# A hybrid mLSTM and sparse-attention block on one core: two sets of transposes alternate between PSUM rings, and one output chunk changes its issuing engine

## The chip, the cores and the metric

The kernel runs on 1 core of one Trainium2 chip. The metric is the device time of one execution in microseconds (us). Three runs of the kernel before gave 654.09, 654.55 and 655.37 us; the median is 654.55 us. A further execution was taken by the profiler; its rows are the ones quoted below.

## The reference, cut to what matters

The block takes `x` (256 tokens of width 2048), normalises it, and projects it into everything that two parallel groups of heads need. At the end it multiplies by gates, projects back, adds a gated per-token embedding and normalises again.

```python
h = rmsnorm(x, norm_g[l])
(mq, mk, mv, mo, mz, mi, mf, nq, kc, vc, ks, vs, kw, vw, ng, nz) = split_cols(h @ w_in[l], IN_SPLITS)
...
hm = head_layernorm(hm, m_norm_g[l]).astype(x.dtype)
m_out = hm * jax.nn.sigmoid(mo) * jax.nn.silu(mz)
q = partial_rope(heads(nq, N_HEADS) * (N_HEAD_DIM ** -0.5), positions)
n_att = nsa_mixer(q, ...)
...
x = x + jnp.concatenate([m_out, n_out], axis=-1) @ w_out[l]
ple = rmsnorm(p[l] @ ple_proj_w[l], ple_norm_g[l])
x = x + jax.nn.sigmoid(x @ ple_gate_w[l]) * ple
return rmsnorm(x, final_norm_g)
```

Two tensors matter here: `q`, the 16 attention heads of 64 that the sparse attention reads, and `hm`, the 4 mLSTM heads of 256 that go, gated, into the output projection. TensorE needs both with the feature on the partitions, so both are transposed on it.

## The kernel before

**Tiles and stages.** All weights come as a stream of 512 KB pieces (units, class `Unit`). Each is loaded by SyncE's DMA queue (line 157), split by ScalarE into a high part `whi` (line 166) and by VectorE into a low part `wlo` (line 167), and multiplied three times: `x_hi*w_hi`, `x_lo*w_hi`, `x_hi*w_lo` (line 193; lines 178 and 181 where the features are on the partitions). These products (`mainps`) fill TensorE. Everything else, the attention, the mLSTM and the gates, is written as Python generators (`tracks`) whose pieces are laid between the units.

**What sets the order.** The order of every engine is the order of the Python code (`manual_schedule`), and each engine works it off strictly. One turn of the main loop emits: the evacuation of a block that ended in the turn before, the load of unit i+4, the split of unit i+3, the products of unit i, and then `advance()`, which lets every live track go on to its next `yield`. A track that yields after its transposes has their evacuation in the next turn, behind that turn's products on TensorE.

**PSUM.** It has 8 banks of 2 KB per partition, dealt out in rings by tag: `main` 3 banks (`main_ps`), `aux` 2 tiles of one bank (`aux`), `wide` 1 tile of two banks (`wide`), `acc` 1. A new tile of a ring may be written when the tile that had its place has been read for the last time; the framework puts that wait on the first TensorE instruction that writes it.

**Queries.** In `nsa` (from line 602) the loop over `h0` handles four heads a turn: 4 transposes (line 625) into two `aux` tiles, then, one turn later, 4 copies by ScalarE (line 614) and 4 subtractions by VectorE (line 619), which read both tiles and write the high and the low part of `qT`. There are 4 such groups, called here q1 to q4, one unit apart. After q4 come the scores of the compressed keys, 2 x 16 small products (line 631), into `psc`, which is a `wide` tile of two banks.

**Mixed heads.** In `gate_m` (from line 1048) the gated `hm` is transposed in groups of 4 (line 1067) into one `aux` tile of one bank each; ScalarE (line 1070) and VectorE (line 1072) evacuate it in the next turn, two instructions each. There are two such tracks, for the two halves of the features, one turn apart, so the four groups come in the order m1 (second half, `k0` = 4), m2 (first half, `k0` = 0), m3 (second half, `k0` = 6), m4 (first half, `k0` = 2); m2 and m3 fall into the same turn and m4 into the next one.

**The end.** The last product block is cut into three (`EDGES`), the second half of the tokens last. `write(t)` (lines 1256 to 1268) scales four chunks of 128 x 512 in the order of columns 1, 0, 3, 2: chunk 1 by VectorE (line 1265), 0 and 2 by ScalarE (line 1267), 3 by VectorE (line 1263). Each is issued to memory by SyncE (line 1268). `write(1)` is the last thing that the program does.

Of the kernel before, what the change touches and what calls it, by code (L numbers as in the profile page):

```python
# [19 lines left out]
S = 256  # L20
# [79 lines left out]
def hybrid_block(ctx, tc, x, xT, pT, positions, wst, cols, w1in, ple_norm_g, final_norm_g, out):  # L100
    nc = tc.nc
# [11 lines left out]
    def aux(shape, dt=F32):  # L113
        return psum.tile(shape, dt, name="auxps", tag="aux", bufs=2)

    def wide(shape):
        return psum.tile(shape, F32, name="wideps", tag="wide", bufs=1)

    def t2(shape, dt=F32, name="t2"):
        return tmp.tile(shape, dt, name=name, tag="t2", bufs=5)  # L120
# [233 lines left out]
    def rope(xv, nh):  # L354
        tt = (t4 if nh > NG else t2)([128, 2, T, nh, ROT], name="rope")
        a, b = tt[:, 0], tt[:, 1]
        c = cos16.rearrange("p t a b -> p t (a b)")
        V.tensor_tensor(a, xv[:, :, :, 0:ROT], c[:, :, None, :].to_broadcast([128, T, nh, ROT]), OP.mult)
        V.tensor_tensor(b[:, :, :, 0:HALF], xv[:, :, :, HALF:ROT],
                        nsin[:, :, None, :].to_broadcast([128, T, nh, HALF]), OP.mult)  # L360
        V.tensor_tensor(b[:, :, :, HALF:ROT], xv[:, :, :, 0:HALF],
                        sin8[:, :, None, :].to_broadcast([128, T, nh, HALF]), OP.mult)
        V.tensor_tensor(xv[:, :, :, 0:ROT], a, b, OP.add)
# [238 lines left out]
    def nsa():  # L602
        nonlocal natt, qT
        while "cmp" not in done:
            yield
        qT = tmp.tile([128, NH, S], F32R, name="qT", tag="qT")
        rope(q.rearrange("p t (h d) -> p t h d", d=ND), NH)
        yield
        prev = None
        for h0 in range(0, NH + 4, 4):  # L610
            if h0:
                for a in range(2):
                    for c in range(2):
                        A.copy(qT[0:ND, h0 - 4 + 2 * a + c], prev[a][c * ND:(c + 1) * ND])
                for a in range(2):
                    for c in range(2):
                        h = h0 - 4 + 2 * a + c
                        src = prev[a][c * ND:(c + 1) * ND]
                        V.tensor_tensor(qT[ND:128, h], src, qT[0:ND, h].bitcast(F32), OP.subtract)
            if h0 < NH:  # L620
                prev = [aux([128, S]) for _ in range(2)]
                for a in range(2):
                    for t in range(T):
                        c0 = (h0 + 2 * a) * ND
                        PE.transpose(prev[a][:, t * 128:(t + 1) * 128], q[:, t, c0:c0 + 2 * ND], ident)
                yield
        natt = tmp.tile([128, NW // 128, S], F32, name="natt", tag="q8")
        psc = wide([128, T, NH, 2, NC16])
        for t in range(T):
            for h in range(NH):  # L630
                PE.matmul(psc[:, t, h].rearrange("p a c -> p (a c)"), qT[:, h, t * 128:(t + 1) * 128],  # L631
                          kcmpT[:, h // NJ].rearrange("p a c -> p (a c)"), start=True, stop=True)
            yield
        pc = t2([128, T, NJ, NG, NC16], name="pc")
        for t in range(T):
            sc = psc[:, t].rearrange("p (g j) a c -> p g j a c", g=NG)
            pg = pc[:, t].rearrange("p j g c -> p g j c")
            V.tensor_tensor(pg, sc[:, :, :, 0], cadd[:, t, None, None, :].to_broadcast([128, NG, NJ, NC16]), OP.add)
            V.tensor_tensor(pg, sc[:, :, :, 1], pg, OP.add)
        tracks.append(cmp_probs(pc))  # L640
        while not {"k0", "k1", "vw"} <= done:
            yield
        yield from attend_all()

    def cmp_probs(pc):
        nonlocal pcT
        pcT = tmp.tile([128, T, NJ, 128], F32R, name="pcT", tag="pcT")
        cst = tmp.tile([128, 2, T, NJ, NG], F32, name="cst", tag="cst")
        a0, a1 = (cst[:, i].rearrange("p t j g -> p (t j g)") for i in range(2))
        pcf = pc.rearrange("p t j g c -> p (t j g) c")  # L650
        V.tensor_reduce(a0, pcf, axis=AX.X, op=OP.max)
        V.tensor_tensor(pcf, pcf, a0[:, :, None].to_broadcast([128, T * NH, NC16]), OP.subtract)
        yield
        A.activation(pcf, pcf, AF.Exp)
        yield
        V.tensor_reduce(a1, pcf, axis=AX.X, op=OP.add)
        V.reciprocal(a1, a1)
        for t in range(T):
            pt = pc[:, t].rearrange("p j g c -> p (j g) c")
            V.tensor_tensor(pt, pt, cmul[:, t, None, :].to_broadcast([128, NH, NC16]), OP.mult)  # L660
        yield
        while "vw" not in done:
            yield
        V.tensor_tensor(cst[:, 1].rearrange("p t j g -> p t g j"), cst[:, 1].rearrange("p t j g -> p t g j"),
                        gates[:, :, :, 0].rearrange("p t (g j) -> p t g j", g=NG), OP.mult)
        V.tensor_tensor(pcf, pcf, a1[:, :, None].to_broadcast([128, T * NH, NC16]), OP.mult)
        yield
        yield
        H = NG * NC16
        for t in range(T):  # L670
            ps = psum.tile([H, NJ, 128], F32, name="pcps", tag="acc", bufs=1)
            for j in range(NJ):
                PE.transpose(ps[:, j], pc[:, t, j].rearrange("p g c -> p (g c)"), ident)
            yield
            A.copy(pcT[0:H, t], ps)
            V.tensor_tensor(pcT[H:128, t], ps, pcT[0:H, t].bitcast(F32), OP.subtract)
            yield
        done.add("pcT")
# [354 lines left out]
    def ev_mz(i):  # L1033
        def f(ps):
            tzs = []
            for t in range(T):
                tz = t2([128, 512], name="tz")
                A.activation(tz, ps[t], AF.Tanh, scale=rh[:, t:t + 1])
                zc = t2([128, 512], name="zc")
                A.copy(zc, ps[t])  # L1040
                V.scalar_tensor_tensor(tz, tz, 1.0, zc, op0=OP.add, op1=OP.mult)
                tzs.append(tz)
            tracks.append(gate_m(i, tzs))
        return f
# [3 lines left out]
    def gate_m(i, tzs):  # L1048
        nonlocal mixm
        for t in range(T):  # L1050
            sl = gmt[:, t, i * 512:(i + 1) * 512]
            V.scalar_tensor_tensor(sl, sl, 1.0, tzs[t], op0=OP.add, op1=OP.mult)
            yield
        while "mlstm" not in done:
            yield
        for t in range(T):
            hs = hm[:, t, 2 * i:2 * i + 2].rearrange("p h d -> p (h d)")
            V.tensor_tensor(hs, hs, gmt[:, t, i * 512:(i + 1) * 512], OP.mult)
            yield
        if i == 0:  # L1060
            mixm = tmp.tile([128, 2, KT // 2, S], F32R, name="mixm", tag="qk")
        hf = hm.rearrange("p t h d -> p t (h d)")
        for k0 in range(4 * i, 4 * i + 4, 2):
            ps = aux([128, 2, S])
            for j in range(2):
                for t in range(T):
                    PE.transpose(ps[:, j, t * 128:(t + 1) * 128], hf[:, t, (k0 + j) * 128:(k0 + j + 1) * 128], ident)
            yield
            for j in range(2):
                A.activation(mixm[:, 0, k0 + j], ps[:, j], AF.Copy, scale=mgcol[:, k0 + j:k0 + j + 1])  # L1070
            for j in range(2):
                V.scalar_tensor_tensor(mixm[:, 1, k0 + j], ps[:, j], mgcol[:, k0 + j:k0 + j + 1],
                                       mixm[:, 0, k0 + j].bitcast(F32), op0=OP.mult, op1=OP.subtract)
        done.add(f"mix{i}")
# [181 lines left out]
    def write(t):  # L1256
        f = frr[:, t:t + 1]
        o = out[0, t * 128:(t + 1) * 128]
        for c in (1, 0, 3, 2):
            sl = slice(c * 512, (c + 1) * 512)  # L1260
            xx = x2[t][:, sl]
            if c == 3:
                V.scalar_tensor_tensor(xx, xx, f, fgb[:, sl], op0=OP.mult, op1=OP.mult)
            elif c == 1:
                V.tensor_scalar(xx, xx, f, None, op0=OP.mult)
            else:
                A.activation(xx, xx, AF.Copy, scale=f)
            nc.sync.dma_start(o[:, sl], xx)


    halves = [(t, a, a + 512) for a in (512, 0) for t in range(T)]
# [27 lines left out]
    ps = wide([128, 2, 128])  # L1299
# [77 lines left out]
```

## Time and profile before

| what | value |
|---|---|
| median of 3 runs | 654.55 us (654.09 to 655.37) |
| the profiled execution, its own time | 655.25 us |
| its span, first to last instruction | 653.5 us |
| TensorE busy | 638.0 us, 98% of the span |
| VectorE busy | 467.0 us, 71% |
| ScalarE busy | 378.8 us, 58% |
| GpSimd busy | 62.2 us, 10% |
| mean granted TensorE clock, share of full speed | 0.996 |

The profiled execution's own time holds its span and 1.75 us around it; it lies 0.7 us above the median of the three runs and inside their spread. A row of the timeline reads: start in us from the span's start, us from its first start to its last end, engine, line of the kernel, operation, what it writes and reads, shape, count, and in brackets the idle time of the engine before it and what ended that. PE is TensorE's products, PEld its weight loads (a transpose has one of each), DVE is VectorE, ACT ScalarE, POOL GpSimd, SPq SyncE's queue.

### The profile page before, as it was taken

What the parts mean: (1) busy time and instruction counts of PE and PEld (TensorE: products, weight loads), DVE (VectorE), ACT (ScalarE), POOL (GpSimd) and SP (SyncE); (2) the same over time, 40 slices, a digit from 0 to 9 for tenths busy, and PEclk for the clock granted to TensorE, in tenths of its full rate; (3) what the DMA queues carried; (4) which work ended last, traced back from release to release, by engine and by line L of the source; (5) the groups of instructions that cost most, each with busy time, mean ns of one, the idle gap of its engine ahead of it and who ended that gap; (6) DMA issues with size and microseconds to landing.
All of it is one profiled execution on the core that took longest, in us unless ns stands there. A gap on an engine that the chain in (4) does not pass through costs nothing.

```text
span 653.5 us, 9104 instructions
## 1 busy us (share of the span) xinstructions
PE 638.0 (98%) x3287; PEld 550.6 (84%) x3287; DVE 467.0 (71%) x712; ACT 378.8 (58%) x655; POOL 62.2 (10%) x70
## 2 busy tenths in 40 slices
PE   7999999999999999999999999999999999999994
PEld 6889999898888888888888888887888888888884
DVE  4669877877776657799998776787755765545564
ACT  5678844746565655767765656677634433444442
POOL 0002240000111112111110000010000000022430
PEclk9999999999999999999999999999999999999998
DMA  8996555546545445454456653455688665556633
GB/s 294 354 345 203 173 149 157 178 149 197 162 161 161 144 147 161 134 157 128 143 180 187 195 185 127 130 178 166 198 286 286 225 210 189 175 181 195 193 95 130
DMA packets 35902, 121.04 MB, mean 185 GB/s; under 512 B 4240, under 2 KB 5008, under 8 KB 35344
## 3 DMA queue, kind: packets, MB, share of 16 engines
q1 hardware_dynamic: 34704, 115.98, 55.9%
q10 hardware_dynamic: 1152, 4.47, 1.9%
q8 instruction: 26, 0.43, 0.3%
q14 instruction: 20, 0.16, 0.1%
HBM read 118.33 MB, written 2.10 MB: 184 GB/s over the span
## 4 chain that ended last, share of the span: by engine, by line
PE 94%; DVE 2%; DMA 1%; issue 1%; ACT 1%; SPq 0%; POOL 0%; ACTq 0%; POOLq 0%; DVEq 0%
PE mainps L193 61%; PE mainps L178 13%; PE mainps L181 7%; PE wideps L193 3%; PE wideps L692 2%; PE auxps L738 2%; DMA wraw<-in_wst_dram 1%; PE po L771 1%; PE po L769 1%; PE wideps L970 1%; PE auxps L441 1%; PE auxps L1204 1%; PE auxps L945 1%; PE wideps L631 1%; ACT whi L166 0%
## 5 line engine op out<-in xcount | busy, mean ns | idle before, releaser
L167 DVE TENSOR_TENSOR wlo<-wraw,whi 128x1024 fp32r<-128x1024 f32 (+3 forms) x214 | 257.8, 1206 | 151.1 <-ACT whi L166 149.0
L166 ACT CAST whi<-wraw 128x1024 fp32r<-128x1024 f32 (+3 forms) x214 | 216.4, 1013 | 183.6 <-PE mainps L193 123.7
L193 PE MATMUL mainps<-whi,hT 128*128 128x512 f32 (+2 forms) x704 | 182.5, 377 | 0.5 <-DVE vst L527 0.3
L193 PEld LDWEIGHTS mainps<-whi,hT 128*128 128x128 f32 x704 | 128.3, 188 | 17.9 <-ACT whi L166 0.8
L178 PE MATMUL mainps<-hT,whi 128*128 128x512 f32 x384 | 105.6, 396 | 0.0
L193 PE MATMUL mainps<-wlo,hT 128*128 128x512 f32 (+2 forms) x352 | 105.0, 373 | 0.5 <-DVE wlo L167 0.5
L178 PEld LDWEIGHTS mainps<-hT,whi 128*128 128x128 f32 x384 | 66.2, 189 | 9.5
L193 PEld LDWEIGHTS mainps<-wlo,hT 128*128 128x128 f32 x352 | 65.6, 188 | 9.9 <-DVE wlo L167 1.0
L193 PE MATMUL mainps<-whi,x2T 128*128 128x512 f32 (+1 forms) x288 | 70.5, 367 | 0.0
L181 PEld LDWEIGHTS mainps<-hT,wlo 128*128 128x128 f32 x384 | 58.8, 189 | 8.2
L181 PE MATMUL mainps<-hT,wlo 128*128 128x256 f32 x384 | 61.0, 281 | 0.0
L193 PEld LDWEIGHTS mainps<-whi,x2T 128*128 128x128 f32 x288 | 50.8, 189 | 8.7
L726 POOL TENSOR_TENSOR pr<-pr,st 128x1024 f32<-128x1024 f32 x12 | 22.9, 1909 | 220.6 <-DVE st L724 195.0
L193 PE MATMUL mainps<-wlo,x2T 128*128 128x512 f32 (+1 forms) x144 | 41.0, 366 | 0.0
L193 PE MATMUL mainps<-whi,mixm 128*128 128x512 f32 x128 | 35.0, 395 | 0.0
L193 PE MATMUL mainps<-whi,mixn 128*128 128x512 f32 x128 | 34.2, 389 | 0.0
L193 PEld LDWEIGHTS mainps<-wlo,x2T 128*128 128x128 f32 x144 | 26.0, 189 | 4.5
L902 DVE SCALAR_TENSOR_TENSOR qk<-cv,csb,qk 128x253 f32<-128x253 f32 (+2 forms) x48 | 28.3, 589 | 1.2
L715 ACT ACTIVATE pr<-wideps,st 128x128 f32<-128x128 f32 (+1 forms) x64 | 26.2, 422 | 4.1 <-DVE st L704 4.0
L193 PEld LDWEIGHTS mainps<-whi,mixn 128*128 128x128 f32 x128 | 24.0, 188 | 5.0
L193 PEld LDWEIGHTS mainps<-whi,mixm 128*128 128x128 f32 x128 | 23.5, 188 | 4.6
L1228 POOL TENSOR_TENSOR x<-x,gth 128x512 f32<-128x512 f32 x6 | 11.2, 1866 | 111.2 <-DVE gth L1227 96.3
(275 smaller groups left out, 704.4 us busy)
## 6 DMA issues: line engine op xcount, KB each, us to landing
wraw<-in_wst_dram SPq DMA_DIRECT2D x179, 512.0 KB, 3.7
wraw<-in_wst_dram SPq DMA_DIRECT2D x24, 400.0 KB, 3.2
wraw<-in_wst_dram SPq DMA_DIRECT2D x8, 392.0 KB, 3.1
xq<-in_x_dram SPq DMA_DIRECT2D x8, 256.0 KB, 9.1
w1raw<-in_w_dram SPq DMA_DIRECT2D x2, 1024.0 KB, 10.5
x<-in_x_dram ACTq DMA_DIRECT2D x4, 512.0 KB, 5.7
out_dram<-x SPq DMA_DIRECT2D x8, 256.0 KB, 2.5
xf<-in_xT_dram SPq DMA_DIRECT2D x3, 512.0 KB, 6.7
```

Of the source, the lines that this page charges most:

```text
L166: A.copy(hi[:, a:z], raw[:, a:z])
L167: V.tensor_tensor(lo[:, a:z], raw[:, a:z], hi[:, a:z].bitcast(F32), OP.subtract)
L178: PE.matmul(o, self.hi[:, j, m * 128:(m + 1) * 128], b.xT(kt, True), start=kt == 0, stop=False, skip_group_check=True)
L181: PE.matmul(o[:, 0], self.lo[:, j, m * 128:(m + 1) * 128], b.xT(kt)[0], start=False, stop=kt == b.nk - 1, skip_group_check=True)
L193: PE.matmul(b.ps[n], xx, (self.hi, self.lo)[part == 2][:, j, a:z], start=kt + part == 0, stop=part == 2 and kt == b.nk - 1)
L441: PE.matmul(ps, movr[:, j].rearrange("p a g c -> p (a g c)"), w[:, j].rearrange("p a h -> p (a h)"), start=j == 0, stop=j == CS - 1)
L692: PE.matmul(ps[:, j], qT[:, g * NJ + j0 + j, t * 128:nk], kT[:, g, hl, :, 0:nk], start=hl == 0, stop=hl == 1)
L715: A.activation(d["pr"][:, j, b], d["ps"][:, j, b], AF.Exp, bias=st[:, 0, j, b:b + 1], accum_out=st[:, 1, j, b:b + 1])
L726: G.tensor_tensor(pf, pf, d["st"][:, 2].rearrange("p j b -> p (j b)")[:, :, None].to_broadcast([128, 2 * jn, nk]), OP.mult)
L738: PE.transpose(pt[:, s, j], d["pr"][:, j, b, s * 128:(s + 1) * 128], ident)
L902: V.scalar_tensor_tensor(y[:, d:S], a[:, 0:S - d], w(j), y[:, d:S], op0=OP.mult, op1=OP.add)
L1228: G.tensor_tensor(x2[t][:, sl], x2[t][:, sl], ths[t], OP.add)
```

## The change

Three edits. First, `nsa` takes the place of q2 and q4 from the `wide` ring (one tile of two banks, a bank for each of the two outputs), and that of q1 and q3 from `aux` as before. Second, `gate_m` takes m3 and m4 (`k0` = 6 and 2) from `wide`, and m1 and m2 from `aux` as before. Third, in `write(1)` the last chunk (columns 2) is issued by ScalarE behind its own scaling, and not by SyncE. No arithmetic is changed, and no instruction is added or taken away but for waits.

```diff
@@ -618,7 +618,11 @@
             if h0 < NH:
-                prev = [aux([128, S]) for _ in range(2)]
+                if h0 % 8:
+                    pw = wide([128, 2, 512])
+                    prev = [pw[:, a, 0:S] for a in range(2)]
+                else:
+                    prev = [aux([128, S]) for _ in range(2)]
                 for a in range(2):
@@ -1061,7 +1065,7 @@
         for k0 in range(4 * i, 4 * i + 4, 2):
-            ps = aux([128, 2, S])
+            ps = (wide if k0 % 4 else aux)([128, 2, S])
             for j in range(2):
@@ -1265,7 +1269,7 @@
                 A.activation(xx, xx, AF.Copy, scale=f)
-            nc.sync.dma_start(o[:, sl], xx)
+            (nc.scalar if t and c == 2 else nc.sync).dma_start(o[:, sl], xx)
```

The instructions keep their order on TensorE, VectorE and ScalarE; what moves are the banks and with them the waits. TensorE, from the transposes of q4 to the first set of scores, before (`auxps` and `wideps` are the two rings, `mainps` the weight products):

```order
L625 MATMUL auxps<-ident,q 128x128 [waits DVE_49,PE_49]
L625 MATMUL auxps<-ident,q 128x128
L193 MATMUL mainps<-whi,hT 128x392 [waits Activation_49]
L193 MATMUL mainps<-whi,hT 128x392 x3
L193 MATMUL mainps<-wlo,hT 128x392 x2
L193 MATMUL mainps<-whi,hT 128x392 x4
L193 MATMUL mainps<-wlo,hT 128x392 x2
L631 MATMUL wideps<-kcmpT,qT 128x32 [waits Activation_49] x12
L631 MATMUL wideps<-kcmpT,qT 128x32 [waits DVE_49]
L631 MATMUL wideps<-kcmpT,qT 128x32 [waits DVE_49,Activation_49]
L631 MATMUL wideps<-kcmpT,qT 128x32 [waits DVE_49]
L631 MATMUL wideps<-kcmpT,qT 128x32 [waits DVE_49,Activation_49]
```

and now:

```order
L629 MATMUL wideps<-ident,q 128x128 [waits DVE_49,PE_49]
L629 MATMUL wideps<-ident,q 128x128 x3
L193 MATMUL mainps<-whi,hT 128x392 [waits Activation_49]
L193 MATMUL mainps<-whi,hT 128x392 x3
L193 MATMUL mainps<-wlo,hT 128x392 x2
L193 MATMUL mainps<-whi,hT 128x392 x4
L193 MATMUL mainps<-wlo,hT 128x392 x2
L635 MATMUL wideps<-kcmpT,qT 128x32 [waits DVE_49,PE_49,Activation_49]
L635 MATMUL wideps<-kcmpT,qT 128x32 [waits Activation_49] x15
```

The wait for VectorE has moved from the 13th score to the first: the scores now write the two banks that held q4, and no later score waits for VectorE any more, so the first one waits for the last of q4's subtractions.

TensorE, from m2 to m4, before:

```order
L1067 MATMUL auxps<-ident,hm 128x128
L1067 MATMUL auxps<-ident,hm 128x128 [waits DVE_49]
L1067 MATMUL auxps<-ident,hm 128x128 x2
L1067 MATMUL auxps<-ident,hm 128x128 [waits DVE_49,PE_49]
L1067 MATMUL auxps<-ident,hm 128x128 x3
L178 MATMUL mainps<-hT,whi 128x512 x4
L181 MATMUL mainps<-hT,wlo 128x256 x4
L178 MATMUL mainps<-hT,whi 128x512 x4
L181 MATMUL mainps<-hT,wlo 128x256 x4
L1067 MATMUL auxps<-ident,hm 128x128 [waits DVE_49,PE_49]
```

and now:

```order
L1071 MATMUL auxps<-ident,hm 128x128
L1071 MATMUL auxps<-ident,hm 128x128 [waits DVE_49]
L1071 MATMUL auxps<-ident,hm 128x128 x2
L1071 MATMUL wideps<-ident,hm 128x128 x4
L178 MATMUL mainps<-hT,whi 128x512 x4
L181 MATMUL mainps<-hT,wlo 128x256 x4
L178 MATMUL mainps<-hT,whi 128x512 x4
L181 MATMUL mainps<-hT,wlo 128x256 x4
L1071 MATMUL wideps<-ident,hm 128x128 [waits DVE_49,PE_49]
```

m3 no longer waits for VectorE; m4 still does, but the tile before it in its ring is now m3's, one unit earlier, where it was m2's.

VectorE over the same stretch, now:

```order
L167 TENSOR_TENSOR wlo<-wraw,whi 128x1024
L1076 SCALAR_TENSOR_TENSOR mixm<-auxps,csb,mixm 128x256 x2
L1094 SCALAR_TENSOR_TENSOR tz<-th,tz 128x512
L1095 TENSOR_TENSOR tz<-tz,natt 128x512
L167 TENSOR_TENSOR wlo<-wraw,whi 128x1024
L1076 SCALAR_TENSOR_TENSOR mixm<-auxps,csb,mixm 128x256 x2
L1076 SCALAR_TENSOR_TENSOR mixm<-wideps,csb,mixm 128x256 x2
L1098 TENSOR_TENSOR mixn<-tz,mixn 128x512
```

Before, the sixth and seventh rows were one, of four instructions reading `auxps`; the order is the same. The two that free m2's tile stand ahead of the two that free m3's.

## Rows read from the trace of the kernel before

**Rows 1.** The page: busy time by engine, and the granted clock in 40 slices.

```profile
PE 638.0 (98%) x3287; PEld 550.6 (84%) x3287; DVE 467.0 (71%) x712; ACT 378.8 (58%) x655; POOL 62.2 (10%) x70
...
PEclk9999999999999999999999999999999999999998
```

**Rows 2.** Who waited for whom, TensorE: us in total, times, longest.

```profile
PE auxps L1067 <- DVE mixm L1072: 1.5, 1, 1.5
...
PE auxps L625 <- DVE qT L619: 1.0, 2, 0.5
```

**Rows 3.** Timeline of TensorE's weight loads, 118 to 132 us.

```profile
121.78 0.20 PEld L625 LDWEIGHTS auxps<-ident,q 128*128 128x128 f32 x2 [0.69 <-PE auxps L625]
...
124.58 0.20 PEld L625 LDWEIGHTS auxps<-ident,q 128*128 128x128 f32 x2 [0.21 <-PE mainps L193]
...
127.81 0.20 PEld L625 LDWEIGHTS auxps<-ident,q 128*128 128x128 f32 x2 [0.68 <-PE auxps L625]
...
130.05 1.93 PEld L631 LDWEIGHTS wideps<-kcmpT,qT 128*128 128x128 f32 x16
```

**Rows 4.** Timeline of VectorE in the same stretch.

```profile
122.71 1.75 DVE L619 TENSOR_TENSOR qT<-auxps,qT 64x256 fp32r<-64x256 f32 x4
124.94 0.98 DVE L167 TENSOR_TENSOR wlo<-wraw,whi 128x784 fp32r<-128x784 f32 x1 [0.48 <-ACT whi L166]
125.94 1.75 DVE L619 TENSOR_TENSOR qT<-auxps,qT 64x256 fp32r<-64x256 f32 x4
127.92 1.23 DVE L167 TENSOR_TENSOR wlo<-wraw,whi 128x1024 fp32r<-128x1024 f32 x1 [0.22 <-ACT whi L166]
129.17 1.79 DVE L619 TENSOR_TENSOR qT<-auxps,qT 64x256 fp32r<-64x256 f32 x4
```

**Rows 5.** Timeline of ScalarE in the same stretch.

```profile
124.06 0.84 ACT L166 CAST whi<-wraw 128x784 fp32r<-128x784 f32 x1 [0.98 <-PE mainps L193]
```

**Rows 6.** Timeline of TensorE's weight loads, 437 to 448 us: m2, m3 and m4.

```profile
440.44 0.47 PEld L1067 LDWEIGHTS auxps<-ident,hm 128*128 128x128 f32 x4
442.58 0.42 PEld L1067 LDWEIGHTS auxps<-ident,hm 128*128 128x128 f32 x4 [1.68 <-issue]
...
445.83 0.42 PEld L1067 LDWEIGHTS auxps<-ident,hm 128*128 128x128 f32 x4
```

**Rows 7.** Timeline of VectorE in the same stretch.

```profile
440.46 1.23 DVE L167 TENSOR_TENSOR wlo<-wraw,whi 128x1024 fp32r<-128x1024 f32 x1 [0.87 <-ACT whi L166]
441.60 0.87 DVE L1072 SCALAR_TENSOR_TENSOR mixm<-auxps,csb,mixm 128x256 fp32r<-128x256 f32 x2
...
444.85 1.65 DVE L1072 SCALAR_TENSOR_TENSOR mixm<-auxps,csb,mixm 128x256 fp32r<-128x256 f32 x4
```

**Rows 8.** Busy time by stretch: PE, PEld, DVE, ACT, POOL (count), clock, DMA share, GB/s.

```profile
440.40:446.50 6.10, 4.63 (x32) 4.07 (x31) 6.01 (x11) 5.31 (x12) 0.00 (x0) 1.00 0.59 177
```

**Rows 9.** Timeline of all engines from 646.5 us: the last scalings and issues.

```profile
647.57 1.33 ACT L1267 ACTIVATE x<-x,frr 128x512 f32<-128x512 f32 x2 [2.30 <-POOL frr L1254]
...
648.09 1.80 SPq L1268 DMA_DIRECT2D out_dram<-x  x4
```

**Rows 10.** Busy time by stretch, columns as in rows 8: the last transfers.

```profile
649.00:650.00 1.00, 0.00 (x0) 0.00 (x0) 0.00 (x0) 0.00 (x0) 0.00 (x0) 0.50 1.04 383
650.00:651.00 1.00, 0.00 (x0) 0.00 (x0) 0.00 (x0) 0.00 (x0) 0.00 (x0) 0.50 1.04 387
651.00:652.00 1.00, 0.00 (x0) 0.00 (x0) 0.00 (x0) 0.00 (x0) 0.00 (x0) 0.50 0.69 254
```

**Rows 11.** Timeline of TensorE at the start: products of 256 columns.

```profile
1.11 3.57 PE L1301 MATMUL wideps<-wz 128*128 128x256 f32 x15 [1.11 <-DVE mh L233]
```

**Rows 12.** Busy time by stretch, columns as in rows 8: around the last products.

```profile
640.00:644.00 4.00, 4.00 (x36) 4.00 (x35) 3.57 (x10) 1.54 (x3) 0.56 (x1) 1.00 0.02 4
...
646.00:648.00 2.00, 0.00 (x0) 0.00 (x0) 1.26 (x6) 0.43 (x1) 0.56 (x1) 0.96 0.93 346
648.00:650.00 2.00, 0.00 (x0) 0.00 (x0) 0.72 (x2) 0.91 (x2) 0.00 (x0) 0.50 0.55 204
```

## The prediction, on record before the change was run

> **What bounds the kernel now.** I read the page first. TensorE is busy for 638.0 of 653.5 us and its clock is granted in full almost everywhere [rows 1]; nearly all of the idle time lies before the first products and after the last. So a change in the middle can win only what TensorE still waits for there, and it loses whatever new wait it puts on TensorE's queue, one for one, since the weight products stand behind it in the same queue and no idle time later takes a delay up.
>
> The list of who waited for whom comes next. In the two places that the change touches TensorE waits for VectorE: once, 1.5 us, before transposes of mixed heads, and twice, together 1.0 us, before transposes of queries [rows 2]. Both are waits for a bank of the `aux` ring that VectorE hasn't finished reading. That is all there is to be won, by this view 2.5 us. The third view is the timeline of the two places, engine by engine. The reader is to see there not only the wait, but how much work VectorE still has between the wait and the next instruction of TensorE that needs it.
>
> **Queries: what is removed.** The weight loads of the transposes show the waits a little longer than the list: 0.69 us in q2, 0.21 in q3, 0.68 in q4 [rows 3]. With q2 and q4 in `wide`, q2 finds a tile that nobody has used since the start; q3 takes the `aux` tiles of q1, read long before; q4 takes the `wide` tile of q2, which VectorE has finished at 122.71 + 1.75 = 124.46 us [rows 4], while q4 can come at the earliest 0.69 + 0.21 before its present 126.9, at 126.0. All three waits go. TensorE would reach the scores 0.69 + 0.21 + 0.68 = 1.58 us earlier: 130.05 - 1.58 = 128.47 us [rows 3].
>
> **Queries: what is added.** The scores are a `wide` tile of both banks, and now the tile before it in the ring is q4's. Their first product waits until VectorE has made the last subtraction of q4; before, only the 13th score needed that. So the question is when VectorE is there. From q2's evacuation on it has a split, q3's evacuation, a split and q4's evacuation to do, in this order: 0.98 + 1.75 + 1.23 + 1.79 = 5.75 us [rows 4]. Its two gaps, 0.48 and 0.22 us, are waits for ScalarE's split, which itself waited 0.98 us for TensorE [rows 5]; with TensorE earlier they close. With 0.02 us between instructions, four times, VectorE ends q4 at 124.46 + 5.75 + 0.08 = 130.29 us, where it ended at 129.17 + 1.79 = 130.96 before. The hand-over to TensorE takes 0.12 us: q4's second half started at 127.81, and the subtraction that it waited for ended at 125.94 + 1.75 = 127.69 [rows 3, 4]. So the scores start at 130.41 us, against 130.05 now: **+0.36 us**. TensorE then stands for 130.41 - 128.47 = 1.9 us in one piece, where it stood three times. The bounds: +0.2 if only the product and not the weight load ahead of it has to wait (the load is then out of the way), +0.5 if the gaps on VectorE close only in part. I take 0.36, as both halves of q4 held the weight load back too [rows 3]. What is queued behind the waiting score is every weight product; ScalarE's next split and VectorE's behind it have work, and nothing of them is on the path.
>
> **Mixed heads: what is removed.** m3 comes straight behind m2 and waits 1.68 us at its weight load [rows 6] until VectorE has read m1's tile (441.60 + 0.87 = 442.47 us, [rows 7]). In `wide` it waits for nothing, and TensorE comes to m4 at 445.83 - 1.68 = 444.15 us.
>
> **Mixed heads: what is added.** m4 now takes m3's tile, and m3 and m4 are only one unit apart. Its four readers on VectorE, two for m2 and then two for m3, run from 444.85 to 444.85 + 1.65 = 446.50 us [rows 7]. Could they run earlier, with m3 transposed earlier? No: VectorE is busy for 6.01 of the 6.10 us from 440.4 to 446.5 [rows 8]. Its work starts with a split at 440.46 that waited for ScalarE [rows 7], and all of that lies ahead of m3, so it isn't moved by m3. m4 then starts at 446.50 + 0.12 = 446.62 us, against 445.83: **+0.79 us**, after standing for 446.62 - 444.15 = 2.5 us. Bounds: +0.6 and +0.9, from the 0.1 us by which the edges of adjoining rows overlap in this view. What is late next is m4's own evacuation, which VectorE did at 448 us behind another split; the weight products lose 0.79 us and nothing gives it back.
>
> **The last chunk.** SyncE issues the four chunks in 1.80 us from 648.09, so 0.45 apart, the last at about 649.45; ScalarE is done with the scaling of that chunk at 647.57 + 1.33 = 648.90 [rows 9]. Issued by ScalarE it can go some 0.5 us earlier. But the 16 DMA engines are full from 649.0 on: shares of 1.04, 1.04 and 0.69 in the three last microseconds, at 383 to 387 GB/s [rows 10]. The four chunks are 1.05 MB, which at 385 GB/s is 2.7 us of transfer, and it starts just before 649.0 with the first chunk. An issue that only joins a full queue earlier doesn't bring its end forward. I cost this edit at **0**; the cover is the transfer of the three chunks ahead, and without that cover it would be worth 0.45. Bounds: -0.5 and +0.3 (a chunk that gets in the way of the one before it, at most half of one chunk's 0.68 us).
>
> The Trainium skill weighs this differently by a little: DMA: Bandwidth & Descriptors, section Issuing engines are not separate DMA queues, says that DMAs from several engines run on the same 16 engines, and that issuing from several saves only the sequencer's time for the issue. By that sentence the edit would bring one issue's time, and the total would come out at 655.25; the shares of 1.04 speak for none of it.
>
> **The sum.** +0.36 + 0.79 + 0 = +1.15 us. The profiled execution had a span of 653.5 us in a time of 655.25, so its like would be a span of about 654.7 in 656.4; set on the median of the runs, which is 0.7 below that execution, 654.55 + 1.15 = **655.7 us**, 0.18% more. I call under 0.2% (1.3 us) no change throughout; it is about what a measurement of this kernel can tell.
>
> **Rivals.**
>
> *The waits just go.* If VectorE had time to spare, or the hand-over of `wide` asked for less than the last reader, the 1.58 and the 1.68 us would be won and nothing given back: 654.55 - 3.26 = 651.3 us. For it: the waits on the `aux` ring are real [rows 2, 3, 6]. Against it: 6.01 of 6.10 us [rows 8], and the 5.75 us of work in a row [rows 4]. Chance 0.10.
>
> *The earlier issue pays.* The last chunk lands 0.45 us earlier: 655.25 us. Against it stand the full engines [rows 10]. Chance 0.10.
>
> *The clock falls, and the change ends slower.* The two long waits, 1.9 us before the scores and 2.5 us before m4, stand where several short ones stood. In the trace the clock did go to half after TensorE had stopped for good: 1.00 while products ran, 0.96 in 646 to 648 us, 0.50 after that [rows 12]. At the start 15 products of 256 columns took 3.57 us, 0.24 each [rows 11]; at the end 36 of them fell into 4.00 us, 0.11 each, so the half level costs one us in two [rows 12]. If the 2.5 us wait sent the clock down for a stretch like that at the start, it would cost half of 3.57, 1.8 us more: 657.5 us. It decides from 0.3 us of half clock on, since 0.16 us are left to the 0.2% bound. Against it: waits of up to 1.68 us left the clock at 1.00 [rows 6, 8]. Chance 0.10. The Trainium skill, TensorE: Matmul & The Clock Gate, section A second HAM failure mode: psum-queue depth-cycling, tells of a kernel in which short waits between bank changes made the clock swing between its two levels. This trace has such short waits at full clock, so far against that rule; by it the time would be this rival's.
>
> That the change doesn't do what it says is not a rival here: banks and waits are seen in the order of the instructions.
>
> **How the numbers follow.** My forecast has 0.70. Its own bounds are 0.2 + 0.6 - 0.5 = +0.3 and 0.5 + 0.9 + 0.3 = +1.7 us, 654.85 to 656.25; the three runs spread by -0.5 and +0.8 around their median, and I add 0.65 on either side, for the half of it that a median keeps and for 0.3 of a wait that I may have put on the wrong engine: 654.2 to 656.9. The rivals at 651.3 and 657.5 stay out; they are the 2 in 10. I draw the lower end on to **653.9**, where one of the two new waits costs nothing and the last chunk pays in full. Slower by over 0.2% (above 655.86) is 0.29 of the forecast's 0.70, for it lies only 0.16 us below that bound, and the clock's 0.10: 0.39. Faster by over 0.2% (below 653.24) is the first rival's 0.10 and 0.01 for the rest: 0.11. No change: 0.50.
>
> **What would show it.** Right: no wait before q2, q3, q4 and m3; a wait of about 1.9 us before the first score, ended by line 623 (the subtraction of `qT`), and one of about 2.5 us before the last transposes of mixed heads, ended by VectorE's `mixm`; VectorE without a gap before both; the DMA share still at 1.04 in the last microseconds, with the last issue 0.5 us earlier and the last landing at the same distance from the first. Wrong: scores or m4 that start without a wait (the first rival), a last landing that comes forward by 0.4 us or more, or a granted clock under 1.00 at 131 or 447 us.

## The result and the profile after

The changed kernel takes **658.56 us** (median of 9 runs, 657.32 to 662.51) beside 655.00 us (653.86 to 656.62, 9 runs) for the kernel before: a ratio of 1.0066, 95% interval 1.0052 to 1.0081 (the two medians alone give 1.0054; the nine executions fall into two groups, told below). It is slower, and lies above the range of the prediction (653.9 to 656.9). The execution that was profiled is the slowest of the nine, 662.51 us with a span of 660.7; the span before was 653.5.

The page first: the span, the busy time and the granted clock in 40 slices, to be held against [rows 1].

```profile
span 660.7 us, 9096 instructions
...
PE 642.2 (97%) x3287; PEld 555.0 (84%) x3287; DVE 467.6 (71%) x712; ACT 378.7 (57%) x655; POOL 61.3 (9%) x70
...
PEclk9999999989999999999999999998999999999997
```

As many products as before are busy for 4.2 us more (642.2 for 638.0). That can't be a wait; and two slices, the ninth (132 to 149 us) and the 28th (446 to 462 us), show an 8 in the clock where [rows 1] has only nines. They lie at the two places of the change.

Below, a stand is a stretch in which TensorE has its next instruction in hand and waits for another engine. The next view is who waited for whom on TensorE (us in total, times, longest), to be held against [rows 2]:

```profile
PE wideps L1071 <- DVE mixm L1076: 2.3, 1, 2.3
PE wideps L635 <- DVE qT L619: 2.1, 1, 2.1
```

The old waits for `aux` are gone, and each place has one long wait for `wide` instead, ended by the instructions of VectorE that the prediction named. Where the queries go is seen in the timeline of all engines from 119 to 141 us (before: [rows 3 to 5]):

```profile
119.12 0.42 PEld L629 LDWEIGHTS auxps<-ident,q 128*128 128x128 f32 x4 [0.65 <-DVE q L363]
...
122.47 1.55 ACT L614 CAST qT<-wideps 64x256 fp32r<-64x256 f32 x4
...
131.69 3.38 PEld L635 LDWEIGHTS wideps<-kcmpT,qT 128*128 128x128 f32 x16 [2.38 <-issue]
131.72 3.46 PE L635 MATMUL wideps<-kcmpT,qT 128*128 128x32 f32 x16 [2.09 <-DVE qT L619]
...
138.67 1.05 ACT L166 CAST whi<-wraw 128x1024 fp32r<-128x1024 f32 x1 [8.30 <-PE mainps L193]
138.72 1.93 PEld L635 LDWEIGHTS wideps<-kcmpT,qT 128*128 128x128 f32 x16
138.90 1.85 PE L635 MATMUL wideps<-kcmpT,qT 128*128 128x32 f32 x16
139.75 1.23 DVE L167 TENSOR_TENSOR wlo<-wraw,whi 128x1024 fp32r<-128x1024 f32 x1 [6.92 <-ACT whi L166]
```

and in VectorE's own timeline, from the split behind q1 to q4:

```profile
122.66 0.98 DVE L167 TENSOR_TENSOR wlo<-wraw,whi 128x784 fp32r<-128x784 f32 x1
124.05 1.73 DVE L619 TENSOR_TENSOR qT<-wideps,qT 64x256 fp32r<-64x256 f32 x4 [0.41 <-ACT qT L614]
...
126.82 1.73 DVE L619 TENSOR_TENSOR qT<-auxps,qT 64x256 fp32r<-64x256 f32 x4
...
129.84 1.73 DVE L619 TENSOR_TENSOR qT<-wideps,qT 64x256 fp32r<-64x256 f32 x4
```

The same stretch before: the first row from the timeline of the weight loads, the others from that of all engines.

```profile
118.17 0.42 PEld L625 LDWEIGHTS auxps<-ident,q 128*128 128x128 f32 x4 [0.65 <-DVE q L363]
...
130.22 1.85 PE L631 MATMUL wideps<-kcmpT,qT 128*128 128x32 f32 x16
...
133.99 1.93 PEld L631 LDWEIGHTS wideps<-kcmpT,qT 128*128 128x128 f32 x16
134.00 1.05 ACT L166 CAST whi<-wraw 128x1024 fp32r<-128x1024 f32 x1 [2.89 <-PE mainps L193]
...
135.08 1.23 DVE L167 TENSOR_TENSOR wlo<-wraw,whi 128x1024 fp32r<-128x1024 f32 x1 [2.71 <-ACT whi L166]
```

The first 16 scores take 3.46 us, before 1.85; the second 16, the same products for the other half of the tokens seven microseconds later, take 1.85. In between nothing is waited for on TensorE, but ScalarE stands for 8.30 us and VectorE for 6.92, before 2.89 and 2.71: the products themselves are slow. The second place, timeline from 445 to 452 us (before: [rows 6, 7]):

```profile
445.20 0.47 PEld L1071 LDWEIGHTS auxps<-ident,hm 128*128 128x128 f32 x4
...
450.39 0.87 DVE L1076 SCALAR_TENSOR_TENSOR mixm<-wideps,csb,mixm 128x256 fp32r<-128x256 f32 x2
...
451.37 0.42 PEld L1071 LDWEIGHTS wideps<-ident,hm 128*128 128x128 f32 x4 [2.47 <-issue]
451.40 0.63 PE L1071 MATMUL wideps<-ident,hm 128*128 128x128 f32 x4 [2.30 <-DVE mixm L1076]
```

The tail, last scaling and the last chunk's issue (before: [rows 9]):

```profile
654.64 1.33 ACT L1271 ACTIVATE x<-x,frr 128x512 f32<-128x512 f32 x2 [2.30 <-POOL frr L1258]
...
656.01 0.38 ACTq L1272 DMA_DIRECT2D out_dram<-x  x1
```

Last, busy time by stretch (columns as in [rows 8]: PE, PEld, DVE, ACT, POOL, then clock, DMA share, GB/s):

```profile
125.00:131.00 6.00, 4.63 (x28) 4.27 (x26) 5.79 (x11) 5.01 (x11) 0.00 (x0) 1.00 0.65 197
...
133.00:139.00 6.00, 6.00 (x25) 6.00 (x24) 0.00 (x0) 0.33 (x1) 0.00 (x0) 0.53 0.29 87
139.00:141.00 2.00, 2.00 (x19) 2.00 (x18) 1.23 (x1) 0.71 (x1) 0.00 (x0) 1.00 0.00 0
...
453.00:457.00 4.00, 4.00 (x17) 3.48 (x16) 1.05 (x3) 1.56 (x3) 0.00 (x0) 0.61 0.41 131
...
656.00:657.00 1.00, 0.00 (x0) 0.00 (x0) 0.00 (x0) 0.00 (x0) 0.00 (x0) 0.50 1.00 363
657.00:658.00 1.00, 0.00 (x0) 0.00 (x0) 0.00 (x0) 0.00 (x0) 0.00 (x0) 0.50 1.03 387
658.00:659.00 1.00, 0.00 (x0) 0.00 (x0) 0.00 (x0) 0.00 (x0) 0.00 (x0) 0.50 0.80 289
```

TensorE's clock is at 0.53 of its full speed from 133 to 139 us and at 0.61 from 453 to 457, that is for the most part at the lower of its two levels (1.2 of 2.4 GHz), behind each of the two new waits. With marks that both traces have, the 7.2 us between the two spans split up as follows (a mark's own delay is what came on top of the mark above it):

| mark | before | after | added here |
|---|---|---|---|
| q1's first weight load | 118.17 | 119.12 | 0.95 |
| first score's weight load | 130.05 | 131.69 | 0.69 |
| second set of scores, weight load | 133.99 | 138.72 | 3.09 |
| m2's weight load | 440.44 | 445.20 | 0.03 |
| m4's weight load | 445.83 | 451.37 | 0.78 |
| last scalings on ScalarE | 647.57 | 654.64 | 1.53 |
| end of the span | 653.5 | 660.7 | 0.13 |

The first line lies ahead of the change; q1's weight load falls anywhere from 117.1 to 119.1 us in the profiles of this study, so it is the execution's and not the change's. What is left are the two waits, 0.69 + 0.78 = 1.47 us, and two stretches of low clock, 3.09 + 1.53 = 4.6 us. The other executions of the changed kernel are faster than this one. The slower ones have the lower mean clock: four at 0.987 to 0.991 take 660.9 to 662.5 us, five at 0.994 take 657.3 to 658.6. So the 4.6 us are what the slowest one lost to the clock, and most lost less.

### The profile page after: what moved, and what is told of

The parts are those of the page before. It is cut to its first block, busy times and chain, and to the rows that moved or that the text cites. A ratio compares the mean times of both kernels' runs of the same rounds, so it can differ in the third digit from the quotient of the medians.

```text
span 660.7 us, 9096 instructions
## 1 busy us (share of the span) xinstructions
PE 642.2 (97%) x3287; PEld 555.0 (84%) x3287; DVE 467.6 (71%) x712; ACT 378.7 (57%) x655; POOL 61.3 (9%) x70
## 4 chain that ended last, share of the span: by engine, by line
PE 77%; DVE 1%; issue 1%; POOL 0%; ACT 0%; POOLq 0%; DVEq 0%
PE mainps L193 48%; PE mainps L178 13%; PE mainps L181 7%; PE wideps L696 2%; PE auxps L742 2%; PE po L775 1%; PE po L773 1%; PE wideps L974 1%; PE wideps L635 1%; PE auxps L1208 1%; PE auxps L949 1%; DVE mixm L1076 0%; POOL pr L730 0%; PE po L766 0%; PE auxps L952 0%
```

## Experiments

My theory after this reading: the waits cost about 1.5 us (forecast: 1.15), and the rest is the clock, which a long stand of TensorE brings down. The rivals: one of the three edits costs something else that the table only shows in that place; or the low clock is a chance event of the executions that has nothing to do with the waits.

**One edit at a time.** Each of these three is the kernel before with one hunk of the change.

```
 e1_queries
+                if h0 % 8:
+                    pw = wide([128, 2, 512])
+                    prev = [pw[:, a, 0:S] for a in range(2)]
...
 e2_mixed
-            ps = aux([128, 2, S])
+            ps = (wide if k0 % 4 else aux)([128, 2, S])
 e3_issue
-            nc.sync.dma_start(o[:, sl], xx)
+            (nc.scalar if t and c == 2 else nc.sync).dma_start(o[:, sl], xx)
```

> Only the first edit: q2 and q4 from the wide ring; the mixed heads and the last issue as before. Theory C (the long single waits send TensorE's clock to half for a stretch, and that is most of the loss): a wait of about 2.1 us before the first score as in the changed kernel, the scores 0.7 us late, and in part of the executions a stretch at half clock behind it that adds 1.5 to 3 us; ratio to the kernel before between 1.001 and 1.005, with executions at two levels. Theory W (the waits alone cost it, the clock is a bystander): +0.7 us in every execution, ratio 1.001.

> Only the second edit: m3 and m4 from the wide ring; the queries and the last issue as before. Theory C: a wait of about 2.3 us before m4, m4 0.8 us late, then a stretch at half clock worth about 1.5 us in most executions: ratio about 1.0035, mean granted clock 0.994. Theory W: +0.8 us, ratio 1.0012, clock 0.996.

> Only the third edit: the last chunk issued by ScalarE. Both theories: no change, ratio 1.000 within 0.001, since the transfers fill the DMA engines to the end; from the last scaling's start to the end of the span 6.0 us as before. If the earlier issue paid: 0.45 us less, ratio 0.9993.

The queries alone: 658.61 us (657.49 to 662.51, 6 runs), ratio 1.0065 [1.0039, 1.0091], as much as the whole change and more than the 1.001 to 1.005 expected. Its timeline of TensorE and one stretch of its clock:

```profile
130.73 3.54 PE L635 MATMUL wideps<-kcmpT,qT 128*128 128x32 f32 x16 [2.08 <-DVE qT L619]
```
```profile
132.00:134.00 2.00, 2.00 (x11) 2.00 (x11) 0.00 (x0) 0.00 (x0) 0.00 (x0) 0.50 0.54 152
```

The wait and the slow scores are there as in the full change. All six executions have a mean clock of 0.994 or less (two of them 0.985), as all nine of the changed kernel do; of the 61 executions of the kernel before that were timed beside the experiments, one does.

The mixed heads alone: 657.05 us (655.07 to 658.16, 12 runs), 1.0021 [1.0010, 1.0031], or 1.4 us [0.7, 2.0], less than the 1.0035 expected. In the profile, timeline of TensorE and clock of the stretch:

```profile
446.81 0.63 PE L1067 MATMUL wideps<-ident,hm 128*128 128x128 f32 x4 [2.26 <-DVE mixm L1072]
```
```profile
452.00:457.00 5.00, 5.00 (x27) 4.27 (x26) 2.79 (x5) 3.86 (x7) 0.00 (x0) 1.00 0.35 107
```

The wait is the one of the full change, 2.26 us beside 2.30, and behind it the clock stays at 1.00. From q1's first weight load to the last scalings this kernel takes 530.23 us, before 529.40: 0.83 more, the wait alone (0.79 forecast). So at this place the same wait doesn't bring the clock down in every execution. How often isn't told by the mean clock. Four of these 12 executions have 0.993 or 0.994, which hints at a fall in some of them; but kernels without a long stand have such executions too (e7, below), and the mean doesn't say where the clock fell.

The issue alone: 655.57 us (11 runs), 1.0007 [0.9998, 1.0017], no difference that can be measured.

**Filling the stands.** e4_fill is the changed kernel with products that nobody reads in the place of the two stands; e8 has only the first filling (9 products), e9 about half of each (5 and 5).

```
+    FILLQ, FILLM = 9, 10
+    def fill(n):
+        ps = psum.tile([128, 512], F32, name="fillps", tag="acc", bufs=1)
+        for _ in range(n):
+            PE.matmul(ps, identr, hT[:, 0].rearrange("p a s -> p (a s)"), start=True, stop=True)
...
+        fill(FILLQ)
         psc = wide([128, T, NH, 2, NC16])
...
+            if k0 == 2:
+                fill(FILLM)
             ps = (wide if k0 % 4 else aux)([128, 2, S])
```

> The changed kernel with products that nobody reads in place of the two waits: 9 products of 512 columns ahead of the first score and 10 ahead of m4, into the free bank of the acc ring. At 0.216 us each they last 1.9 and 2.2 us, so TensorE comes to both places hardly later than the data. Theory C: the clock stays at 1.00 at both places, and what is left is the two late starts, 0.7 + 0.8 = 1.5 us: ratio 1.002, clock 0.996, executions at one level. Theory W: as the changed kernel or slower by the products that overshoot, ratio 1.006.

656.41 us (655.25 to 658.04, 12 runs), 1.0021 [1.0012, 1.0029]. TensorE's timeline at the two places, and the clock behind them:

```profile
128.62 2.29 PE L124 MATMUL fillps<-hT,identr 128*128 128x512 f32 x9
...
130.84 1.93 PE L643 MATMUL wideps<-kcmpT,qT 128*128 128x32 f32 x16
...
444.93 2.50 PE L124 MATMUL fillps<-hT,identr 128*128 128x512 f32 x10
...
447.39 0.63 PE L1081 MATMUL wideps<-ident,hm 128*128 128x128 f32 x4
```
```profile
131.00:139.00 8.00, 8.00 (x57) 7.96 (x57) 4.10 (x8) 1.77 (x4) 0.00 (x0) 1.00 0.42 135
...
452.00:457.00 5.00, 5.00 (x26) 4.21 (x26) 3.36 (x5) 3.61 (x7) 0.00 (x0) 1.00 0.34 107
```

The scores and m4 come no earlier relative to q1, since they still wait for VectorE, but TensorE doesn't stand, and the clock is at 1.00 at both places. From q1 to the last scalings it takes 530.81 us, 1.41 more than before, near the 1.47 that the two waits add in the changed kernel. The difference between 1.0066 and 1.0021, about 2.9 us (2.4 by the medians), is what the low clock costs in the timed executions. Eleven of the twelve have a mean clock of 0.995 to 0.997, as the kernel before has; the twelfth is the profiled one, with 0.993, whose clock fell at the start of the kernel (see e7). This settles the two rivals: the low clock at these places is the stands' doing, and the edits have no third cost that can be measured.

> The changed kernel with products that nobody reads only ahead of the first score (9 of 512 columns); the wait of about 2.3 us before m4 stays. If the fall of the clock that costs most is the one behind the scores: ratio 1.002 to 1.003, close to the run with both places filled (1.0021), and the clock falls at most in some executions behind m4. If the one behind m4 costs most: ratio 1.005.

657.42 us (656.87 to 658.25, 5 runs), 1.0036 [1.0023, 1.0049]. The profile shows the clock at 1.00 behind both places, and m4's wait unfilled:

```profile
447.93 0.63 PE L1079 MATMUL wideps<-ident,hm 128*128 128x128 f32 x4 [2.30 <-DVE mixm L1084]
```

Three executions have a clock of 0.997, two of 0.992 and 0.994. That would fit a fall behind m4 in some of them, but the ratio lies between the two expectations (1.002 to 1.003 and 1.005) and its interval overlaps e4's, so what the second place costs in the timed executions isn't told apart here.

> The changed kernel with 5 products that nobody reads ahead of the first score and 5 ahead of m4, in place of 9 and 10: about 1.1 us of the wait is filled, and about 1.1 us of standing is left at each place, less than the 1.7 us that the kernel before stood ahead of m3 without a fall of the clock. Theory C, by the length of a single stand: the clock stays up at both places, ratio 1.002 as with both filled, clock 0.995 to 0.997. If any wait at these places brings the clock down: ratio 1.004 to 1.007, clock 0.994 and less.

657.27 us (656.03 to 662.17, 10 runs), 1.0041 [1.0024, 1.0058], more than the 1.002 of theory C. TensorE's timeline and the clock:

```profile
129.69 1.93 PE L643 MATMUL wideps<-kcmpT,qT 128*128 128x32 f32 x16 [0.88 <-DVE qT L626]
...
133.26 1.51 PE L200 MATMUL mainps<-whi,hT 128*128 128x392 f32 x4
...
447.75 0.63 PE L1081 MATMUL wideps<-ident,hm 128*128 128x128 f32 x4 [1.09 <-DVE mixm L1086]
```
```profile
130.00:132.00 2.00, 2.00 (x18) 2.00 (x18) 0.80 (x1) 0.00 (x0) 0.00 (x0) 0.96 0.43 131
...
132.00:134.00 2.00, 2.00 (x8) 2.00 (x7) 0.00 (x0) 0.00 (x0) 0.00 (x0) 0.50 0.65 236
```

In this execution a stand of 0.88 us was enough: the scores still ran at full clock (1.93 us), and the clock fell behind them. At m4 a stand of 1.09 us left it at 1.00. So the length of a stand alone doesn't decide; this was the miss of my expectation. Five of the ten executions have a mean clock of 0.996, as the kernel before, so with the shorter stands the clock probably didn't fall in all of them.

**One tile or two.** e6 has only the queries' edit, but gives q2 and q4 two separate tiles, the bank of `acc` and `wide`, where the change has one tile for both outputs. Held against e1:

```
                 if h0 % 8:
                     pw = wide([128, 2, 512])
-                    prev = [pw[:, a, 0:S] for a in range(2)]
+                    pa = psum.tile([128, S], F32, name="accq", tag="acc", bufs=1)
+                    prev = [pa, pw[:, 0, 0:S]]
```

> Only the queries, and the two outputs of q2 and of q4 lie in two tiles (one of the acc ring, one of the wide ring) and not in one wide tile. Theory: in the changed kernel VectorE's first subtraction of q2 waits 0.41 us for ScalarE's last copy, because both outputs are one tile. Here it waits for the copies of the first output alone: no gap ahead of q2's subtractions, and the first score starts 12.2 to 12.3 us after the first transposes of q1 (12.57 in the changed kernel, 11.88 before). If the gap has another cause: 12.5 to 12.6 us.

One execution: 659.69 us. In the timeline of VectorE and of the weight loads:

```profile
122.12 0.86 DVE L619 TENSOR_TENSOR qT<-accq,qT 64x256 fp32r<-64x256 f32 x2
123.01 0.86 DVE L619 TENSOR_TENSOR qT<-wideps,qT 64x256 fp32r<-64x256 f32 x2
...
129.78 1.86 PEld L636 LDWEIGHTS wideps<-kcmpT,qT 128*128 128x128 f32 x16 [1.98 <-ACT whi L166]
```

VectorE starts on q2 without a wait, where in the changed kernel it waits 0.41 us for the last of ScalarE's copies (122.47 + 1.55 = 124.02) because both outputs are one tile. From q1's weight load (117.58) to the first score it is 12.20 us, against 131.69 - 119.12 = 12.57 in the changed kernel and 11.88 before. With two tiles the scores are late by 0.32 us, the forecast's 0.36; the shared tile adds 0.37. The clock fell here too, about a microsecond behind the scores, and stayed at 0.50 over the second set (3.43 us) until about 143 us.

**Taking the waits away.** e5 is the changed kernel with one more unit of weight products ahead of the scores and one ahead of m4 (a `yield` hands over to them); e10 is the same with all chunks issued by SyncE.

```
                 yield
+        yield
         natt = tmp.tile([128, NW // 128, S], F32, name="natt", tag="q8")
...
+            if k0 == 2:
+                yield
             ps = (wide if k0 % 4 else aux)([128, 2, S])
```

> The changed kernel with one more turn of the main loop ahead of the scores and one ahead of m4, so that a unit of weight products lies where TensorE stood. If the loss comes from the hand-over of the wide ring and from what the long waits do to the clock: both waits gone or under 0.3 us, clock 0.996, and now the waits of the kernel before are really won: 1.6 + 1.7 - 0.2 = about 3 us less than the kernel before, ratio 0.9955. If alternating the rings itself costs something (another bank, a slower reader): ratio 1.000 or above.

> The run with one more turn ahead of the scores and of m4, and the last chunk issued by SyncE as in the kernel before. The last chunk is hidden behind the transfers of the three others either way: the same as with ScalarE's issue, ratio 0.9955 within 0.001. If ScalarE's issue costs or gains something: 0.9948 or 0.9962.

e5: 651.78 us (651.55 to 653.11, 5 runs), **0.9955** [0.9943, 0.9967]. e10: 652.41 us (651.33 to 652.80, 5 runs), 0.9962 [0.9949, 0.9974]; who issues the last chunk makes no difference that can be told. TensorE's timeline in e5, and the stretch ahead of the scores:

```profile
130.20 1.93 PE L636 MATMUL wideps<-kcmpT,qT 128*128 128x32 f32 x16
...
444.93 0.60 PE L1074 MATMUL wideps<-ident,hm 128*128 128x128 f32 x4
```
```profile
125.00:131.00 6.00, 6.00 (x40) 5.72 (x38) 5.79 (x11) 4.66 (x8) 0.00 (x0) 1.00 0.58 191
```

No wait stands in brackets at either place, TensorE is busy for all of the 6.00 us (4.63 in the changed kernel), and the scores themselves, small as they are, don't bring the clock down in this profile. From q1 to the last scalings it takes 526.16 us, 3.24 less than before (e10: 526.19). That is the sum of the old waits, 1.58 + 1.68 = 3.26 us, which the prediction gave to its first rival. Both versions beat both kernels.

**Other banks instead.** e7 leaves the order alone and gives q4 and m4 the bank of `acc`, so that neither stands before a tile in use.

```
+                elif h0 == 12:
+                    pw = psum.tile([128, 2, S], F32, name="accq", tag="acc", bufs=1)
+                    prev = [pw[:, a] for a in range(2)]
...
+            if k0 == 2:
+                ps = psum.tile([128, 2, S], F32, name="accm", tag="acc", bufs=1)
```

> q2 and m3 from the wide ring as in the changed kernel, but q4 and m4 from the one bank of the acc ring, which is free at both times; the last issue by ScalarE. No hand-over of the wide ring is left: scores 1 to 8 wait for nothing of VectorE, and m4 waits for nothing. By the theory of the hand-over: both long waits gone, at most 0.4 us of waits among the later scores, clock 0.996, 2.8 to 3.2 us less than the kernel before, ratio 0.9955. If TensorE's earlier arrival is taken back elsewhere: ratio 0.998 to 1.000.

653.77 us (652.75 to 655.39, 12 runs), 0.9981 [0.9972, 0.9990]: faster than before, by less than half of what was expected. Its profile shows two waits of 0.2 us among the scores and no low clock at either place, only one at the start of the kernel, ahead of anything that the edit touches: 0.57 from 8 to 12 us, behind a wait of 1.26 us for the first weights (e4's profile has one there too, 0.62, behind a wait of 1.83; the kernel before has 1.00 behind 1.47, the changed one 1.00 behind 1.70). From q1 to the last scalings the profile takes 526.86 us, 2.54 less than before, so at the places of the edit most of what was expected is there. But 7 of the 12 executions have a mean clock of 0.990 to 0.994, and where it fell in those isn't seen in the one profile. Why the timed executions show no more than 0.9981 stays open.

## Why the prediction was wrong

*What bounds the kernel:* right. Each wait that was put on TensorE's queue came out at the end: between the two places, over 300 us, the delay changed by 0.03 us, and taking the waits away without new ones (e5) gave back what [rows 3, 6] had promised. One reading was too strong: of the 15.5 us in which TensorE is idle, some 5.7 lie between the start of the first products at 1.11 us and the end of the last at 644.85, so it isn't "nearly all" outside; no term of the sum rests on it.

*Queries, removed:* right. No wait is left before q2, q3 and q4.

*Queries, added:* right in kind, too small. Forecast +0.36 us, measured +0.69. The term behind it that was wrong is "VectorE has finished at 122.71 + 1.75": I took the start of q2's subtractions from [rows 4], where the outputs are two tiles and VectorE can begin on the first while ScalarE still copies the second. The diff makes them one tile, and VectorE waited until ScalarE was through with it. e6 shows it: 0.32 us with two tiles. The bounds (+0.2 to +0.5) didn't hold the value, since they were drawn around the hand-over and the gaps, and not around this. The prediction named a VectorE without a gap as a sign of being right; those 0.41 us are the gap.

*Mixed heads:* right, +0.78 us for +0.79 forecast, with a stand of 2.47 us at the weight load for 2.5, and 0.83 in e2's profile.

*The last chunk:* right, 0. It was issued 656.01 - 654.64 = 1.37 us behind the start of the last scalings, 0.5 earlier than before (649.45 - 647.57 = 1.88, by the prediction's estimate of that issue), and the span ended 6.06 us behind that start, before 5.93: the DMA engines were full at shares of 1.00 and 1.03 as in [rows 10]. e3's 1.0007 [0.9998, 1.0017] agrees. The Trainium skill (DMA: Bandwidth & Descriptors, section Issuing engines are not separate DMA queues) says that issuing from several engines saves only the sequencer's time for the issue; here the issue came 0.5 us earlier and the end did not.

*The sum without the clock:* 1.47 us in the profile and 1.0021, some 1.4 us, in e4, for 1.15 forecast. With the clock up, as in e4 (656.41 us), the time lies in the range. So the waits were mis-sized by 0.3 us, and that alone would not have been a miss.

*The clock: this is the step that failed.* I had it as a rival at 0.10, slower at 657.5 us, and placed it behind m4's wait, the longer one. The argument against it was "waits of up to 1.68 us left the clock at 1.00". It took the length of one wait at one place for a rule. The runs showed in its place that a stand ahead of the scores, even a shorter one, is followed by half clock. There the clock fell in all four profiles of kernels that stand (after, e1, e6, e9, with waits of 2.09, 2.08, 1.7 and 0.88 us at the first score), and in none of the eight that don't stand there for longer than about 0.2 us. Behind m4 a stand of 2.26 to 2.30 us brought it down in one profile (after) and not in two (e2, e8); the stand ahead of m3 (1.47 to 1.48 us at the product, 1.67 to 1.68 at its weight load) left it up in all four profiles that have it (before, e1, e3, e6). What differs in view between the two places is what follows: at the scores 16 products of 32 columns, at m3 and m4 four transposes and then full weight products. That this is the reason is my inference. No run put full products behind a stand at the scores, or small ones behind m4's.

The price was mis-sized too: 1.8 us, against 3.09 us at the scores and 1.53 at m4. It was taken from 15 products at the start, where the trace grants 1.00 and not half clock, so that row doesn't show the price of the clock. Nor is there one price: from the first score's weight load to m2's it took 3.12 us (after), 3.16 (e1), 4.71 (e6) and 1.50 us (e9) longer than before, and as long as before in e4. The wait that I thought harmless was the dear one.

The Trainium skill, TensorE: Matmul & The Clock Gate, section A second HAM failure mode: psum-queue depth-cycling, tells of a kernel in which frequent short stands between bank changes make the clock swing. The prediction held [rows 6, 8] against it. After the runs this case agrees with it in part: at the scores a single stand of 0.88 us was followed by half clock, and at q2, q3, q4 and m3 before the change stands of 0.2 to 1.68 us left the clock at 1.00. I should have given that rule a larger chance.

## What to carry to other kernels

Alternating between two rings takes a wait from one user and hands it to the next user of the borrowed tile: look at who takes that tile next and when its last reader is done, and count a tile that holds two outputs as free, and as readable, only as a whole. Where TensorE is the bound, several short waits merged into one long one can cost more than their sum, since the clock may go down behind it: here some 2.9 us on top of 1.5 us of waits. A forecast needs the clock as a term of its own there. It was worst where small products followed; whether they are the reason wasn't tested. One unit of other work between the producer and the wait (e5) was worth more than any choice of banks: 0.9955 against 0.9981 and 1.0066.

## What was not expected of the hardware

- TensorE's clock went to its lower level although the engine had work in every instant after the stand: in 133 to 139 us it was busy for 6.00 of 6.00 us, with a granted clock of 0.53. Sixteen products of 32 columns then took 3.46 us for 1.85.
- The scores without a stand left the clock at 1.00 (e4, e5), and stands of up to 1.68 us between full products did too [rows 6, 8]. A stand of 2.30 us between full products brought it down in one profile of three.
- The fall isn't the same in every execution. Behind m4 the same wait went either way, and in the changed kernel's nine executions the mean clock was anything from 0.987 to 0.994. At the start of the kernel it fell behind waits of 1.83 us (e4) and 1.26 us (e7), and not behind 1.47 us (before) or 1.70 us (after). What decides it is open.
- A low clock on TensorE shows as waits elsewhere: ScalarE stood for 8.30 us and VectorE for 6.92, where they stood for 2.89 and 2.71 before. Neither is a cause; TensorE waited for neither.
